# The sample's attention and heads in other steps of a two-layer hybrid decoder step

## The chip, the cores and the metric

The kernel runs on one core of one Trainium2 chip. The metric is device time in microseconds (us) of one execution, lower is better. Engines: TensorE (PE, its weight loads PEld), VectorE (DVE), ScalarE (ACT), GpSimd (POOL), and SyncE (SP), which here issues every load and store as one queue, in order. The granted clock of TensorE is given as a share of its full 2.4 GHz.

## The reference, cut to what matters

Two layers, each with a prompt of 2048 tokens and a "sample" of 8 sequences with 4 tokens each, on the same weights (D_MODEL 1024):

```
z = rms(x) @ w_in                       # 1024 -> 3336 columns
att = sink attention (window 128: the prompt banded, the sample against its cache) * silu(gate_a)
dn  = gated delta rule over conv(q, k, v): chunks of 64, a unit triangular solve per
      chunk and head, then a scan over the chunks; rms norm * silu(gate_d)
y = x + concat(att, dn) @ w_out
```

The prompt has 32 chunks and four delta heads. The sample runs the same formulas on its cached keys and its recurrent state. Layer 2 needs layer 1's sample output as its input, so layer 1's sample work has to be done before layer 2's sample products begin. Layers are called 0 and 1 below.

## The kernel before, in words

The prompt is worked in groups of 512 tokens: four groups a layer, g0 to g3 for layer 0, g4 to g7 for layer 1, one after the other. A group is 68 steps. Each step takes a piece of the weights (two in each of the first four) and issues 12 main products with it (24 in the first four, L484; each fp32 product is three, on high and low halves). The steps by block: 0–3 k, v and the delta coefficients; 4–11 the delta branch's k; 12–19 the attention's q; 20–27 the delta q; 28–35 the delta v; 36–43 the delta gate; 44–51 the attention gate; 52–67 w_out.

Weights: in the first group of a layer the raw piece is loaded (L259) and split into `hl` by ScalarE (L262) and GpSimd (L263), and hl goes to DRAM (L273). The other groups load hl back (L265, 512 KB a piece). Piece n is used in step n − 4 (from piece 8 on). hl has five buffers, so the load of piece n waits until TensorE is done with piece n − 5, which is step n − 9. In the rows of the order below, `hl_4884<-hl0_34_1603` is the load of piece 34 of layer 0.

All else hangs on these steps. `tk.add(gen, n, s, e)` spreads the n parts of a generator over steps s to e, and the table W holds the numbers. In which row an instruction then stands on its engine is settled when the program is built, by a scheduler that also weighs when each buffer comes free: small tiles come from shared pools (f2, nine buffers; f4, five).

For each group one chain is of weight: the gate products (L607), pre (L762 to L781: its matrices AK), stores to `ad` (L788), two loads At on SP (L805), 31 rows of the triangular inverse on GpSimd (L811, L813), X (L817), the store xd and the loads Xc and Xd on SP (L824 to L829), and on TensorE the first product that joins the inverse's blocks, L840, called p1 below. What follows needs the inverse: more joins, the scan over chunks, the norm and gate, and w_out's second half.

The sample's work stands between. `SampleProducts` (L519) multiplies the sample's x with each raw piece. Sample attention, pre (its conv and gates) and four heads (`sample_head`) follow. Its output products (smT, L519 again) need the raw pieces of w_out. The heads' matmuls are those of L1275 to L1343, sample attention is L1097 to L1169, sample pre L1193 to L1247.

The lines that this turns on:

```
add(inv_rows(), 33, W["ir0"], W["ir1"][gi])
add(inv_task(), 6, W["iv0"][gi], W["iv1"][gi])
...
hl = wp.tile([P, 2, kk, m], F32R, tag="hl", name="hl", bufs=W["wla"] + 1)
...
dma(At[r], ad.rearrange("a b j i -> (a b) j i"))
...
dma(xd.rearrange("a b i j -> (a b) i j"), X)
Xd = f2([P, NC, 32], name="Xd")
dma(Xd, xd.rearrange("a b i j -> (b i) a j"))
```

Of the kernel before, what the change touches and what calls it, by code (L numbers as in the profile page):

```python
# [18 lines left out]
P = 128  # L19
# [3 lines left out]
NB_S = 8  # L23
# [8 lines left out]
NG = SEQ // T  # L32
# [12 lines left out]
C_END = 512  # L45

W = dict(k1=8, pre0=13, pre1=19, q0=17, q1=30, ir0=20, ir1=((32,) + (27,) * 3), iv0=(36, 31, 31, 31), iv1=(41, 36, 36, 36), att0=24, att1=47,
         qk0=29, qk1=35, sc0=(41,) * 4, sc1=52, sa0=-4, sa1=30, sp0=20, sp1=50, sh0=58, shd=11, shl=13, wla=4, wraw=3, xn0=2, xn1=8, sla=3,
         md0=53, md1=55, ma0=45)


R3 = 3 * TS
# [89 lines left out]
def hybrid_kernel(ctx, tc, a):  # L142
# [20 lines left out]
    def f4(shape, dt=F32, name="f4"):  # L163
        return f4p.tile(shape, dt, tag="f4", name=name, bufs=5)

    def f2(shape, dt=F32, name="f2"):
        return f2p.tile(shape, dt, tag="f2", name=name, bufs=9)
# [7 lines left out]
    def xt_(shape):  # L175
        return ps_x.tile(shape, F32, tag="x", name="px")
# [30 lines left out]
    def silu2(out, z, n, m):  # L207

        th = f2([P, m], name="th")
        A.activation(th[:n], z, AF.Tanh, scale=0.5)  # L210
        V.scalar_tensor_tensor(out, th[:n], 1.0, z, op0=ALU.add, op1=ALU.mult)
# [22 lines left out]
    def pieces():  # L234
        for l in range(DEPTH):
            stash = []
            for gi in range(NG):
                for n, (src, out) in enumerate(pieces_of(l)):
                    if gi == 0:
                        kk, m = src.shape[1:]  # L240
                        stash.append(dr.tile([P, 2, kk, m], F32, name=f"hl{l}_{n}"))
                    yield src, stash[n], gi == 0, gi == 0 or (gi == 2 and out)

    wsrc = pieces()
    wready = []

# [30 lines left out]
    tk = Tasks()  # L277
# [253 lines left out]
    def sample_projections(L, sT):  # L531
        zcol = [0]

        def zstore(zt):
            n = zt.shape[1]
            dma(L.zs[:, zcol[0]:zcol[0] + n], zt)
            zcol[0] += n

        return SampleProducts(sT, [(W0C, 1, zstore)] + [(256, 2, zstore) if feat else (512, 1, zstore) for feat, _ in BLOCKS])
# [529 lines left out]
    def s1(shape, nm):  # L1069
        return smt(shape, nm, 1)  # L1070
# [190 lines left out]
    def sample_head(L, h):  # L1261
        l, zs, n = L.l, L.zs, TS
        kT, qT, vT = (y[:, h] for y in L.kqv)
        hs = slice(h, h + 1)
        hw = f2([R3, 4, P], name="hw")
        r, o = hw[:, 0], hw[:n, 3:4]
        S0 = f4([P, NB_S, P], name="S0")
        dma(S0, a["state_delta"][l, :, h].rearrange("b k v -> k b v"))
        dg = f2([n, P], name="dgs")
        dma(dg, zs[:, Z_DG + h * P:Z_DG + (h + 1) * P])  # L1270
        sel = f2([P, 2, P], name="sel")
        dma(sel, a["const_k"])
        yield
        pa = xt_([n, 2, n])
        PE.matmul(pa[:, 0], kT[:, 0:n], kT[:, 0:n], start=True, stop=True)  # L1275
        PE.matmul(pa[:, 1], kT[:, 0:n], qT[:, 0:n], start=True, stop=True)
        AKs = s1([n, 2, 3, n], "AKs")
        for i in range(2):
            V.scalar_tensor_tensor(AKs[:, i], pa[:, i].unsqueeze(1).to_broadcast([n, 3, n]), L.scc[:n, hs],
                                   L.dec[:, h].unsqueeze(1).to_broadcast([n, 3, n]), op0=ALU.mult, op1=ALU.mult)  # L1280
        V.tensor_mul(AKs[:, 0], AKs[:, 0], cs_s[:n, S_STR:S_STR + n].unsqueeze(1).to_broadcast([n, 3, n]))
        kq = f2([P, NB_S, 32], name="kq")
        G.memset(kq, 0.0)
        for i, y in enumerate((kT, qT)):
            V.tensor_copy(kq[:, :, LS * i:LS * i + LS], y.rearrange("p (b l) -> p b l", l=LS))
        kv3 = f2([P, 2, 3, n], name="kv3")
        A.copy(kv3[:, 0], kT.unsqueeze(1).to_broadcast([P, 3, n]))
        A.copy(kv3[:, 1], vT.unsqueeze(1).to_broadcast([P, 3, n]))
        yield

        pkq = xt_([P, 2, P])
        for b in range(NB_S):
            r0 = 32 * (b % 4)
            PE.matmul(pkq[r0:r0 + 32, b // 4], kq[:, b], S0[:, b], start=True, stop=True, tile_position=(0, r0))
        kqs = f2([P, 2, P], name="kqs")
        A.copy(kqs, pkq)
        yield
        pt = xt_([P, 3, P])
        for hb in range(2):
            PE.matmul(pt[:, 0], sel[:, hb], kqs[:, hb], start=(hb == 0), stop=(hb == 1))  # L1300
        for i in range(2):
            PE.transpose(pt[:R3, 1 + i], kv3[:, i].rearrange("p a b -> p (a b)"), ident)
        V.tensor_scalar(r, pt[:R3, 2], L.ssqv[:, hs], None, op0=ALU.mult)
        V.scalar_tensor_tensor(r, pt[:R3, 0], L.neG[:, hs], r, op0=ALU.mult, op1=ALU.add)
        V.tensor_copy(o[:, 0], pt[R3:, 0])
        V.tensor_scalar(o[:, 0], o[:, 0], L.eG[:n, hs], None, op0=ALU.mult)
        kd = f2([R3, P], name="skd")
        V.tensor_scalar(kd, pt[:R3, 1], L.sck[:, hs], None, op0=ALU.mult)
        kd3 = wk.tile([R3, P], F32R, tag="kd3", name="kd3", bufs=1)
        V.tensor_copy(kd3, kd)  # L1310
        V.tensor_sub(kd3[n:2 * n], kd[n:2 * n], kd3[n:2 * n].bitcast(F32))
        yield
        w = r
        for i in range(LS - 1):
            pm = xt_([R3, P])
            PE.matmul(pm, AKs[:, 0].rearrange("p a b -> p (a b)"), w[:n], start=True, stop=True)
            w2 = hw[:, 1 + i % 2]
            V.tensor_sub(w2, r, pm)
            w = w2
            yield  # L1320
        pm = xt_([n, P])
        PE.matmul(pm, AKs[:, 1, 0], w[:n], start=True, stop=True)
        V.tensor_add(o[:, 0], o[:, 0], pm)
        w3 = wk.tile([R3, P], F32R, tag="w3", name="w3", bufs=1)
        V.tensor_copy(w3, w)
        V.tensor_sub(w3[2 * n:3 * n], w[2 * n:3 * n], w3[2 * n:3 * n].bitcast(F32))
        wbd = f4([R3, NB_S, P], F32R, name="wbd")
        V.tensor_mul(wbd, w3.bitcast(F32).unsqueeze(1).to_broadcast([R3, NB_S, P]),
                     BM.unsqueeze(2).to_broadcast([R3, NB_S, P]))
        yield  # L1330
        for hb in range(2):
            pu = xt_([P, 4, P])
            PE.matmul(pu, kd3, wbd[:, 4 * hb:4 * hb + 4], start=True, stop=True)
            for b in range(4):
                bb = 4 * hb + b
                V.scalar_tensor_tensor(S0[:, bb], S0[:, bb], L.glb[:, h, bb:bb + 1], pu[:, b], op0=ALU.mult, op1=ALU.add)
        dma(a["s_delta"][l, :, h].rearrange("b k v -> k b v"), S0)
        gate = f2([n, 1, P], name="sgate")
        silu2(gate[:, 0], dg, n, P)
        delta_out(o, L.srq[:n, hs], L.srq2[:n, hs], gate, o, n)  # L1340
        yield
        pt = xt_([P, n])
        PE.transpose(pt, o[:, 0], ident[:n, :n])  # L1343
        A.activation(L.smT[:, 4 + h], pt, AF.Copy, scale=L.dngh)
        yield


    xT, sx, x = [], [], []
    lgen = layer(0)
    L = next(lgen)  # L1350
    sg = sx_stage(L, sx)
# [20 lines left out]
    for l in range(DEPTH):  # L1372
        for gi in range(NG):
            at = tk.at
            if gi == 1:
                tk.add(sample_att(L), 10, at + W["sa0"], at + W["sa1"])
                tk.add(sample_pre(L), 11, at + W["sp0"], at + W["sp1"])
                for h in range(4):
                    s = at + W["sh0"] + W["shd"] * h
                    tk.add(sample_head(L, h), 10, s, s + W["shl"])  # L1380
            if gi == 0:
                sg = sample_projections(L, sx[0])
            g = group(L, gi, xT, sg if gi == 0 else None)
            at, xT, x, Ln, gn = tk.at, [], [], L, gi + 1
            if gi == NG - 1 and l < DEPTH - 1:
                lgen = layer(l + 1)
                Ln, gn = next(lgen), 0
                sx = []
                tk.add(sx_stage(Ln, sx), 4, at + 10, at + 16)
                tk.add(lgen, 1, at + 4, at + 8)  # L1390
            if gn < NG:
                tk.add(x_norm(Ln, gn, x), 7, at + W["xn0"], at + W["xn1"])
                for kh in range(2):
                    tk.add(x_scale(Ln, kh, x, xT), 4, at + 11 + 4 * kh, at + 15 + 2 * kh)
            out_proj(L, gi, g, L.smT if gi == 2 else None)
            L = Ln


# [61 lines left out]
```

## Time and profile before

| | |
|---|---|
| median of 3 runs | 2385.87 us (2385.57 to 2388.23) |
| profiled execution | 2384.89 us |
| its span (first to last instruction) | 2383.1 us |
| TensorE, VectorE, ScalarE, GpSimd busy | 93%, 69%, 38%, 19% |
| mean granted clock of TensorE | 0.972 |
| longest and shortest group | g0 318.9 us, g3 274.2 us |

The groups follow each other without a gap, so the time is the sum of their lengths, plus 21.5 us before the first main product. Times of instructions are counted from the span's start.

### The profile page before, as it was taken

What the parts mean: (1) busy time and instruction counts of PE and PEld (TensorE: products, weight loads), DVE (VectorE), ACT (ScalarE), POOL (GpSimd) and SP (SyncE); (2) the same over time, 40 slices, a digit from 0 to 9 for tenths busy, and PEclk for the clock granted to TensorE, in tenths of its full rate; (3) what the DMA queues carried; (4) which work ended last, traced back from release to release, by engine and by line L of the source; (5) the groups of instructions that cost most, each with busy time, mean ns of one, the idle gap of its engine ahead of it and who ended that gap; (6) DMA issues with size and microseconds to landing.
All of it is one profiled execution on the core that took longest, in us unless ns stands there. A gap on an engine that the chain in (4) does not pass through costs nothing.

```text
span 2383.1 us, 41057 instructions
## 1 busy us (share of the span) xinstructions
PE 2227.7 (93%) x14340; PEld 1771.6 (74%) x14340; DVE 1642.2 (69%) x5060; ACT 909.6 (38%) x2864; POOL 447.4 (19%) x732
## 2 busy tenths in 40 slices
PE   6989999879999899979999899999899989999799
PEld 5766788658887687867877677887688777788677
DVE  6677677577678764677656867778767787557663
ACT  3544523234233342334325445244432344323331
POOL 3272320400004000040023623104000130002100
PEclk9989999979999999989999999999999999999899
DMA  5654685514765348544566546854357534675236
GB/s 172 208 190 160 206 282 184 158 57 140 225 194 170 105 146 267 181 124 131 162 213 222 173 148 215 272 190 125 118 162 224 192 113 133 200 231 161 82 116 199
DMA packets 211298, 414.14 MB, mean 174 GB/s; under 512 B 61340, under 2 KB 89604, under 8 KB 211028
## 3 DMA queue, kind: packets, MB, share of 16 engines
q1 hardware_dynamic: 211092, 411.53, 53.4%
q8 instruction: 113, 1.85, 0.3%
q14 instruction: 93, 0.76, 0.1%
HBM read 312.84 MB, written 101.62 MB: 174 GB/s over the span
## 4 chain that ended last, share of the span: by engine, by line
PE 59%; DVE 8%; POOL 6%; DMA 3%; issue 2%; ACT 2%; SPq 0%; POOLq 0%; ACTq 0%; DVEq 0%
PE mm L484 40%; POOL Xh L813 3%; POOL pr L811 3%; PE px L711 2%; PE px L946 1%; PE px L954 1%; PE px L940 1%; PE px L926 1%; PE px L934 1%; PE px L701 1%; PE px L781 1%; DMA hl<-hl 1%; PE px L668 1%; PE px L519 1%; DVE vT L744 1%
## 5 line engine op out<-in xcount | busy, mean ns | idle before, releaser
L484 PE MATMUL mm<-xT,hl 128*128 128x512 f32 x3072 | 777.5, 403 | 4.1 <-POOL hl L263 3.8
L484 PEld LDWEIGHTS mm<-xT,hl 128*128 128x128 f32 x3072 | 571.0, 192 | 124.2 <-issue 6.7
L484 PE MATMUL mm<-hl,xT 128*128 128x512 f32 (+1 forms) x2304 | 511.2, 369 | 44.3 <-DVE rs_t L204 25.9
L484 PEld LDWEIGHTS mm<-hl,xT 128*128 128x128 f32 x2304 | 379.1, 192 | 114.4 <-issue 56.5
L263 POOL TENSOR_TENSOR hl<-raw,hl 128x512 fp32r<-128x512 f32 (+1 forms) x144 | 186.5, 1300 | 409.7 <-ACT hl L262 360.2
L811 POOL TENSOR_TENSOR pr<-At,Xh 128x126 f32<-128x126 f32 (+22 forms) x248 | 99.2, 400 | 580.1 <-DMA At<-ad 286.6
L484 PE MATMUL mm<-mixA,hl 128*128 128x512 f32 x768 | 187.9, 397 | 0.0
L484 PE MATMUL mm<-mixD,hl 128*128 128x512 f32 x768 | 181.6, 392 | 1.0 <-DVE mixD L970 1.0
L1029 POOL TENSOR_TENSOR mixA<-m,mixA 128x256 fp32r<-128x256 f32 x64 | 45.5, 736 | 719.2 <-ACT mixA L1028 492.7
L484 PEld LDWEIGHTS mm<-mixD,hl 128*128 128x128 f32 x768 | 142.6, 188 | 33.7 <-DVE mixD L970 1.8
L744 DVE SCALAR_TENSOR_TENSOR KQ<-mm,pc,KQ 128x511 f32<-128x511 f32 (+2 forms) x192 | 142.0, 740 | 35.1 <-ACT KQ L741 34.8
L484 PEld LDWEIGHTS mm<-mixA,hl 128*128 128x128 f32 x768 | 140.7, 188 | 30.4 <-issue 2.2
L262 ACT CAST hl<-raw 128x512 fp32r<-128x512 f32 (+1 forms) x144 | 85.0, 595 | 140.2 <-PE mm L484 76.4
L689 ACT ACTIVATE Pt<-Pt,nm 128x128 f32<-128x128 f32 x256 | 99.3, 391 | 21.5 <-DVE nm L681 21.5
L813 POOL TENSOR_TENSOR Xh<-Xh,pr 128x126 f32<-128x126 f32 (+22 forms) x248 | 103.0, 416 | 18.9
L1060 DVE TENSOR_TENSOR xr<-mm,xr 128x512 f32<-128x512 f32 x64 | 43.7, 691 | 79.6 <-PE mm L484 79.6
L672 ACT COPY Pt<-px 128x256 f32<-128x256 f32 x128 | 43.7, 374 | 143.1 <-PE px L669 110.8
L704 DVE TENSOR_TENSOR PT<-px,cst 128x512 f32<-128x512 f32 x124 | 82.1, 683 | 16.7 <-PE px L701 16.2
L701 PE MATMUL px<-cst,Pt 128*128 128x128 f32 x256 | 41.9, 289 | 41.2 <-ACT th L210 26.9
L741 ACT ACTIVATE KQ<-mm,pc 128x512 f32<-128x512 f32 x64 | 43.7, 687 | 94.0 <-PE mm L484 93.9
L668 PE MATMUL px<-kT,q 128*128 128x256 f32 (+1 forms) x256 | 72.6, 313 | 5.0 <-DVE q L650 1.7
L359 ACT CAST xT<-x 128x512 fp32r<-128x512 f32 x64 | 35.5, 618 | 93.9 <-PE mm L484 83.0
(392 smaller groups left out, 3708.7 us busy)
## 6 DMA issues: line engine op xcount, KB each, us to landing
hl<-hl SPq DMA_DIRECT2D x512, 512.0 KB
hl<-hl SPq DMA_DIRECT2D x64, 264.0 KB
raw<-in_wf_dram SPq DMA_DIRECT2D x64, 256.0 KB
raw<-in_w_out_dram SPq DMA_DIRECT2D x64, 256.0 KB
x<-in_x_prompt_dram SPq DMA_DIRECT2D x16, 512.0 KB
raw<-in_wt_dram SPq DMA_DIRECT2D x32, 256.0 KB
xr<-in_x_prompt_dram SPq DMA_DIRECT2D x32, 256.0 KB
y<-xr SPq DMA_DIRECT2D x32, 256.0 KB
```

The lines of the kernel that those rows point to most:

```text
L262: A.copy(hl[:, 0], raw)
L263: G.tensor_sub(hl[:, 1], raw, hl[:, 0].bitcast(F32))
L484: PE.matmul(pss[u], lhs, rhs, start=(k == 0 and q == 0), stop=(k == 7 and q == 2))
L668: PE.matmul(sps[kv][:, jj, c0:], q, kT[:, kv, cols], start=True, stop=False)
L689: A.activation(Pt[:, kv, j], Pt[:, kv, j], AF.Exp, bias=nm[:, h:h + 1], scale=0.125, accum_out=den[:, h:h + 1])
L701: PE.transpose(pt[:, j, :], Pt[:, kv, j], ident)
L704: V.tensor_mul(ptt, pt, (umat if kb else slower).unsqueeze(1).to_broadcast([P, 4, P]))
L711: PE.matmul(po[kv * HD:kv * HD + HD, :], vts[tt + kb][:, kv * HD:kv * HD + HD], PT[kv, kb].rearrange("p a b -> p (a b)"), start=(kb == 0 o ...
L744: V.scalar_tensor_tensor(dest[:, d:], ps[:, 0:T - d], w, dest[:, d:], op0=ALU.mult, op1=ALU.add)
L811: G.tensor_mul(pr, At[:, j, j + 1:].unsqueeze(2).to_broadcast([P, n, m]), Xh[:, j, 0:m].unsqueeze(1).to_broadcast([P, n, m]))
L813: G.tensor_sub(Xh[:, j + 1:, 0:m], Xh[:, j + 1:, 0:m], pr)
L1029: G.tensor_sub(lo, m, hi.bitcast(F32))
```

## The change

- Sample attention, pre and heads of layer l now run from group l + 1 of the layer (g1 in layer 0, g6 in layer 1); before, from group 1 in both (g1, g5). In layer 0, attention and pre are spread over other, earlier steps (`sa1` 30 to 12, `sp0`, `sp1` 20, 50 to 8, 24), and the heads start 57, 66, 125 and 134 steps after the group's start, so two in each of the next two groups, each over 11 steps (before 58, 69, 80, 91, over 13). In layer 1 they start at 57, 66, 75 and 84. All those steps are clear of the blocks of v and the delta gate (28 to 43).
- The sample's input products of layer 1 move from g4 to g5. There the weights are not split, so the raw pieces are loaded once more, beside hl (13.4 MB).
- The output products move from the third group of a layer to the last (g2 to g3, g6 to g7), with their raw loads.
- The sample's x of layer 1 (`sx_stage`) is set up in steps 24 to 40 of g4, instead of 10 to 16 of g3.
- In each head five f2 tiles (kq, kv3, kqs, skd, dgs) are packed into two (kqv, kqd).

```diff
-         ... sa1=30, sp0=20, sp1=50, sh0=58, shd=11, shl=13, ...
+         ... sa1=12, sp0=8, sp1=24, sh=((57, 66, 125, 134), (57, 66, 75, 84)), shl=11, sx0=24, sx1=40, ...
...
-                    yield src, stash[n], gi == 0, gi == 0 or (gi == 2 and out)
+                    yield src, stash[n], gi == 0, gi in (0, 3) if out else gi in (0, l)
...
-        dg = f2([n, P], name="dgs")
+        kqv = f2([P, 512], name="kqv")
+        kq = kqv[:, 0:256].rearrange("p (b l) -> p b l", l=32)
+        kv3 = kqv[:, 256:448].rearrange("p (i a b) -> p i a b", i=2, a=3)
+        kqd = f2([P, 512], name="kqd")
+        kqs = kqd[:, 0:256].rearrange("p (a b) -> p a b", a=2)
+        kd, dg = kqd[:R3, 256:384], kqd[:n, 384:512]
...
-            if gi == 1:
+
+            if gi == l + 1:
                 tk.add(sample_att(L), 10, at + W["sa0"], at + W["sa1"])
                 tk.add(sample_pre(L), 11, at + W["sp0"], at + W["sp1"])
                 for h in range(4):
-                    s = at + W["sh0"] + W["shd"] * h
+                    s = at + W["sh"][l][h]
                     tk.add(sample_head(L, h), 10, s, s + W["shl"])
-            if gi == 0:
-                sg = sample_projections(L, sx[0])
-            g = group(L, gi, xT, sg if gi == 0 else None)
+            if gi == 0 and l == 1:
+                sx = []
+                tk.add(sx_stage(L, sx), 4, at + W["sx0"], at + W["sx1"])
+            sg = sample_projections(L, sx[0]) if gi == l else None
+            g = group(L, gi, xT, sg)
...
-            out_proj(L, gi, g, L.smT if gi == 2 else None)
+            out_proj(L, gi, g, L.smT if gi == NG - 1 else None)
```

The rows move as follows at the three places that the prediction speaks of.

On SP in g1, before, around the two At loads (hl0_33 is piece 33 of layer 0):

```order
L265 DMA hl_4713<-hl0_31_1441 128x1024
L265 DMA hl_4742<-hl0_32_1476 128x1024
L265 DMA hl_4798<-hl0_33_1534 128x1024
L805 DMA At_4509<-ad_4159 64x1024
L265 DMA hl_4884<-hl0_34_1603 128x1024
L805 DMA At_4509<-ad_4159 64x1024
L265 DMA hl_4948<-hl0_35_1685 128x1024
```

and of the change:

```order
L265 DMA hl_5583<-hl0_42_2111 128x1024
L265 DMA hl_5705<-hl0_43_2212 128x1024
L265 DMA hl_5728<-hl0_44_2252 128x1024
L788 DMA ad_4298<-AK_4297 32x4x32 x4
L805 DMA At_4663<-ad_4298 64x1024 x2
L824 DMA xd_5326<-X_5046 64x1024
L828 DMA Xc_5330<-xd_5326 32x16x32
L829 DMA Xc_5330<-xd_5326 32x16x32
L826 DMA Xd_5328<-xd_5326 128x16x32
L265 DMA hl_5748<-hl0_45_2321 128x1024
```

Both At loads move behind the load of piece 44, ten pieces later, and the store and loads of the inverse's result follow at once.

On SP in g5, before, around the same loads (hl1 is layer 1):

```order
L265 DMA hl_17048<-hl1_28_13809 128x1024
L788 DMA ad_16682<-AK_16681 32x4x32
L265 DMA hl_17101<-hl1_29_13866 128x1024
L805 DMA At_17032<-ad_16682 64x1024
L265 DMA hl_17155<-hl1_30_13898 128x1024
L805 DMA At_17032<-ad_16682 64x1024
L265 DMA hl_17236<-hl1_31_13964 128x1024
```

and of the change, with the raw pieces between:

```order
L265 DMA hl_16953<-hl1_31_13761 128x1024
L259 DMA raw_16992<-in_wf_dram 128x512
L805 DMA At_16774<-ad_16412 64x1024
L259 DMA raw_17053<-in_wf_dram 128x512
L265 DMA hl_16994<-hl1_32_13786 128x1024
L265 DMA hl_17055<-hl1_33_13839 128x1024
L259 DMA raw_17125<-in_wf_dram 128x512
L805 DMA At_16774<-ad_16412 64x1024
```

The second At load moves from piece 30 to piece 33, and behind raw loads.

On TensorE in g1, before, from the group's first block on (96 products of 264 columns are steps 0 to 3, then 12 a step):

```order
L484 MATMUL mm<-hl,xT 128x264 x96
L484 MATMUL mm<-xT,hl 128x512 x33
L607 MATMUL px<-cst,gx 128x128
L617 MATMUL px<-g,cst 128x16
L618 MATMUL px<-g,ones 128x16
L484 MATMUL mm<-xT,hl 128x512 x15
```

and of the change:

```order
L484 MATMUL mm<-hl,xT 128x264 x72
L1097 MATMUL px<-cst,qks 128x32
L1099 MATMUL px<-cst,qks 128x32 x4
L484 MATMUL mm<-hl,xT 128x264 x24
L484 MATMUL mm<-xT,hl 128x512 x96
L484 MATMUL mm<-hl,xT 128x512 x3
L1112 MATMUL px<-cst,kc 128x128 x8
L607 MATMUL px<-cst,gx 128x128
```

The gate product L607 moves behind the sample attention's key transposes, from 33 main products into the K block to 99, the first of step 12.

## Rows read from the trace of the kernel before

**Rows 1.** The page: the span, and busy time, share and instructions by engine.

```profile
span 2383.1 us, 41057 instructions
...
PE 2227.7 (93%) x14340; PEld 1771.6 (74%) x14340; DVE 1642.2 (69%) x5060; ACT 909.6 (38%) x2864; POOL 447.4 (19%) x732
```

**Rows 2.** Windows, groups g0 to g7; columns as printed in the first line.

```profile
core 0: us, PE busy (x) PEld busy (x) DVE busy (x) ACT busy (x) POOL busy (x), PEclk, DMA share, GB/s
21.50:340.40 318.90, 294.72 (x1999) 225.42 (x2000) 223.50 (x580) 144.27 (x418) 121.95 (x141) 0.96 0.59 201
340.40:645.20 304.80, 280.39 (x1740) 226.16 (x1738) 206.36 (x707) 104.74 (x346) 31.84 (x73) 0.94 0.49 157
645.20:940.50 295.30, 283.14 (x1824) 223.54 (x1824) 213.57 (x697) 105.83 (x349) 34.22 (x75) 0.98 0.56 175
940.50:1214.70 274.20, 258.05 (x1589) 212.77 (x1587) 183.15 (x558) 101.15 (x325) 34.03 (x75) 0.98 0.52 162
1214.70:1527.60 312.90, 292.32 (x2023) 222.50 (x2023) 216.90 (x572) 142.66 (x415) 122.25 (x141) 0.97 0.60 201
1527.60:1812.30 284.70, 274.30 (x1741) 221.55 (x1739) 206.84 (x704) 105.02 (x346) 32.66 (x73) 0.99 0.52 164
1812.30:2107.60 295.30, 283.13 (x1823) 223.72 (x1823) 213.56 (x697) 105.76 (x349) 35.27 (x75) 0.98 0.55 174
2107.60:2383.10 275.50, 255.81 (x1564) 210.80 (x1562) 165.20 (x506) 91.38 (x304) 31.25 (x72) 0.97 0.48 152
```

**Rows 3.** Timeline of SP's issues, g1, g2, g4, g5, g7: start, us, instruction.

```profile
430.36 0.48 SPq L805 DMA_DIRECT2D At<-ad  x1
...
462.21 0.32 SPq L265 DMA_DIRECT2D hl<-hl  x1
...
475.45 0.48 SPq L829 DMA_DIRECT2D Xc<-xd  x1
...
491.36 0.38 SPq L826 DMA_DIRECT2D Xd<-xd  x1
...
724.74 0.46 SPq L805 DMA_DIRECT2D At<-ad  x1
...
1308.70 0.47 SPq L805 DMA_DIRECT2D At<-ad  x1
...
1601.19 0.47 SPq L805 DMA_DIRECT2D At<-ad  x1
...
2178.30 0.45 SPq L805 DMA_DIRECT2D At<-ad  x1
```

**Rows 4.** Timeline of TensorE at p1 in the same groups: start, us, instruction.

```profile
498.41 1.20 PE L840 MATMUL px<-Xd,AK 32*32 32x32 f32 x64
...
791.22 1.20 PE L840 MATMUL px<-Xd,AK 32*32 32x32 f32 x64
...
1401.27 1.20 PE L840 MATMUL px<-Xd,AK 32*32 32x32 f32 x64
...
1665.74 1.14 PE L840 MATMUL px<-Xd,AK 32*32 32x32 f32 x60
...
2245.08 1.20 PE L840 MATMUL px<-Xd,AK 32*32 32x32 f32 x64 [0.25 <-DMA Xd<-xd]
```

**Rows 5.** Windows: g1 before p1; first 20 steps of g2, g3; eight steps.

```profile
462.20:490.20 28.00, 9.70 (x41) 7.66 (x41) 20.84 (x63) 12.97 (x54) 2.95 (x5) 0.59 0.17 42
...
645.20:718.60 73.40, 73.40 (x452) 60.32 (x451) 56.40 (x229) 26.42 (x95) 0.62 (x2) 1.00 0.68 204
...
940.50:1005.30 64.80, 64.46 (x380) 55.70 (x379) 38.51 (x146) 23.85 (x80) 0.00 (x0) 1.00 0.63 200
...
952.30:975.80 23.50, 23.16 (x107) 18.95 (x107) 17.29 (x74) 7.77 (x17) 0.00 (x0) 1.00 0.66 214
```

**Rows 6.** Groups of instructions by line, L519: busy us, mean ns.

```profile
L519 PE MATMUL px<-raw,sxT 128*32 128x128 f32 (+1 forms) x896 | 48.0, 288 | 0.8 <-DMA raw<-in_wf_dram 0.5 <-DMA raw<-in_w_dram 0.4
...
L519 PE MATMUL px<-raw,smT 128*32 128x128 f32 x256 | 12.8, 283 | 0.5 <-DMA raw<-in_w_out_dram 0.5
```

More of the change, by code (lines that the diff above doesn't have):

```diff
@@ L47 @@
 W = dict(k1=8, pre0=13, pre1=19, q0=17, q1=30, ir0=20, ir1=((32,) + (27,) * 3), iv0=(36, 31, 31, 31), iv1=(41, 36, 36, 36), att0=24, att1=47,
-         qk0=29, qk1=35, sc0=(41,) * 4, sc1=52, sa0=-4, sa1=30, sp0=20, sp1=50, sh0=58, shd=11, shl=13, wla=4, wraw=3, xn0=2, xn1=8, sla=3,
+         qk0=29, qk1=35, sc0=(41,) * 4, sc1=52, sa0=-4, sa1=12, sp0=8, sp1=24, sh=((57, 66, 125, 134), (57, 66, 75, 84)), shl=11, sx0=24, sx1=40, wla=4, wraw=3, xn0=2, xn1=8, sla=3,
          md0=53, md1=55, ma0=45)
@@ L1281, in sample_head @@
         V.tensor_mul(AKs[:, 0], AKs[:, 0], cs_s[:n, S_STR:S_STR + n].unsqueeze(1).to_broadcast([n, 3, n]))
-        kq = f2([P, NB_S, 32], name="kq")
         G.memset(kq, 0.0)
@@ L1285, in sample_head @@
             V.tensor_copy(kq[:, :, LS * i:LS * i + LS], y.rearrange("p (b l) -> p b l", l=LS))
-        kv3 = f2([P, 2, 3, n], name="kv3")
         A.copy(kv3[:, 0], kT.unsqueeze(1).to_broadcast([P, 3, n]))
@@ L1294, in sample_head @@
             PE.matmul(pkq[r0:r0 + 32, b // 4], kq[:, b], S0[:, b], start=True, stop=True, tile_position=(0, r0))
-        kqs = f2([P, 2, P], name="kqs")
         A.copy(kqs, pkq)
@@ L1306, in sample_head @@
         V.tensor_scalar(o[:, 0], o[:, 0], L.eG[:n, hs], None, op0=ALU.mult)
-        kd = f2([R3, P], name="skd")
         V.tensor_scalar(kd, pt[:R3, 1], L.sck[:, hs], None, op0=ALU.mult)
@@ L1387, in hybrid_kernel @@
                 Ln, gn = next(lgen), 0
-                sx = []
-                tk.add(sx_stage(Ln, sx), 4, at + 10, at + 16)
                 tk.add(lgen, 1, at + 4, at + 8)
```

## The prediction

> **What bounds the kernel now.** The page comes first: TensorE is busy for 93% of the span, VectorE for 69%, GpSimd for 19% [rows 1]. That looks like a kernel that its matmuls pace, and for most of a group they do. The table by group is read next [rows 2]: every group has the same 864 main products, yet the lengths go from 274.2 us (g3) to 318.9 us (g0). Two things make the difference. Part is more work on TensorE (the busy column: 258.05 in g3, 283.14 in g2). The rest is time in which it stands still: length less busy is 139.7 us over the eight groups (2361.6 less 2221.9, the sums of the two columns), 24.4 in g1, 10.4 in g5, 24.2 and 20.6 in g0 and g4.
>
> To see what TensorE waits for, follow one chain: the second At load on SP, then 31 rows of the inverse on GpSimd, X, xd, Xd, and the first join product p1 (L840) on TensorE. The starts are in [rows 3] and [rows 4]. From At to p1 it takes 68.0 us in g1 (430.36 to 498.41), 66.5 in g2, 64.5 in g5 and 66.8 in g7; g3 and g6 have the form of g7 and g2. Where the weights are split it takes 92.6 (g4), since GpSimd also does the subtractions of the split (122.25 us busy there, against 31 to 35 elsewhere [rows 2]). So the window is nearly the same whatever else a group does: who moves the At load moves p1, and TensorE cannot go past p1, as its queue is in order. From p1 to the group's end it is 146.8 us in g1, 149.3 in g2, 126.3 in g4, 146.6 in g5 and 138.0 in g7 (group ends from [rows 2]). A group is thus three stretches: start to At, the window, and the tail.
>
> That the window does stop TensorE is seen in g1: in the 28 us from 462.20 it is busy for 9.70, and the granted clock is 0.59, which is a mix of 2.4 GHz (1.0) and 1.2 GHz (0.5) [rows 5].
>
> **Prices.** A sample head's matmul: the first 20 steps of g2 take 73.40 us and those of g3 64.80 [rows 5]; they differ by 41 sample matmuls, so 8.6/41 = 0.21 us each, evictions and waits included. The sample's output products are 12.8 us busy over both layers, 6.4 us a layer; its input products are 48.0, so 24 a layer [rows 6]. Little hides them, since they stand in TensorE's queue between main products and TensorE is busy there for 73.40 of 73.40 us.
>
> **The change group by group** (all against the profiled execution, 2384.89 us, 0.04% below the median of 2385.87).
>
> *g0* is the same program: 0.
>
> *g1: +26.* The sample's attention and pre are now spread over steps up to 24 and its heads are gone. That should help TensorE; the order says otherwise. The gate product L607 moves from step 6 to 12, the prompt's pre products from 13–19 to 19–32, and SP issues both At loads behind the load of piece 44, not around that of piece 34 (the first place of the order). SP is in order, and piece 44's load needs the buffer of piece 39, which TensorE frees at the end of step 35. Before, that load left at 462.21 [rows 3]. After, some 30 small matmuls (transposes and scores of q) that stood ahead of it follow it; at the 0.1 to 0.2 us above that is about 5 us, so 457 (452 to 465). Then four small stores to ad, which At reads, and the two At loads: about 6 us by the distances of such issues, At at 463 instead of 430.36. With 66 to 68 us of window p1 stands at 530, 31 later. The tail loses 19 sample matmuls, 4 us: 146.8 − 4. Sum 31.6 − 4 = +27; at the lower end of the window (66) +26, which I take. Were piece 44 no obstacle, the last pre product in step 32 (10 us earlier) would hold At at about 453, and the sum would be +16.
>
> *g2: −12, g3: +11.* The output products leave g2 for g3, and of the heads two stand in each, by 20 and 22 matmuls in the order that reach into them, with At back where g3 has it now, behind piece 30. g2 = g3 of before with 42 sample matmuls: 274.2 + 42·0.21 = 283.0, against 295.3. g3 = 274.2 + 22·0.21 + 6.4 = 285.2.
>
> *g4: −22.* The 24 us of input products leave. The split stays, so the window stays at 92.6 and only what stood before At and in the tail is saved, but that is nearly all: idle of 20.6 us (312.9 − 292.3) bounds what may be swallowed. Range −17 to −38, the latter if the idle time of this group, too, came from the products.
>
> *g5: +17.* It gets the 24 us of products and the raw weights again, 13.4 MB, and loses sample attention and heads. At stands behind pieces 31 and 33 and two raw loads, thus three steps later (second place of the order): 3·2.94 us (the eight steps from 952.30 take 23.50 [rows 5]), 120 of the 224 products stand ahead of At, at 24/224 = 0.107 us each 12.8, some 25 sample matmuls fewer are −5: +16.7. Window 66.5 rather than 64.5: +2. Tail: 64 products come (6.9), 43 sample matmuls go (9.0): −2. Range +12 to +31, the upper end if the raw loads make the weights late. Their room: 164 GB/s over 284.7 us is 46.7 MB; with 13.4 more in 302 us it is 199 GB/s, and g0 moves 201 [rows 2]. That is the only evidence on contention, and it bounds the cost: g0 is also the group with the longest window.
>
> *g6: −1.* Sample attention and pre of layer 1 come, with one head; output products (6.4) go; the order has 100 sample matmuls there instead of 62, 38 at 0.1 to 0.21 are about 5. The order of its inverse stays.
>
> *g7: +20.* The heads and the output products come; the order of its SP and TensorE reads like that of g2 of before, so 295.3 against 275.5.
>
> Sum: 26 − 12 + 11 − 22 + 17 − 1 + 20 = +39, so **2424 us**. Total work is the same but for the second raw load; what is lost is g1's window, which is opened 33 us late with nothing left to fill it. The moves of the other groups nearly cancel (+13).
>
> **Rivals.**
>
> *The window shrinks (other side).* The change packs five f2 tiles of each head into two (kqv, kqd), and in g1 the order has xd, Xc, Xc and Xd in one piece. Before, in g1, Xd is issued at 491.36, 15.9 us after the second Xc at 475.45 [rows 3]: SP waited for a buffer. If it now leaves at once, each window shrinks, by at most 15.9 us. Seven groups take part (all but g0); it decides from 39/7 = 5.6 us each, and 10 us each give 2354. Against it: Xd in the order of after still waits for VectorE and TensorE, which release its buffer. The Trainium skill, "Perfetto Trace Analysis", section "Optimization Strategy", says that the same gap repeated can mean too few buffers; here a gap of the same size does repeat, but no row shows that the buffer is the packed tiles'.
>
> *TensorE sets the time.* Its main products do not change, and it is at 93% [rows 1]. If its queue has enough to do in the longer g1 window, work moves and the sum does not: 2384.9 ± 5. For it: all that is moved is TensorE work that exists in both programs. Against it: lengths in [rows 2] do not go with busy time (g3 and g5, 16.2 busy apart, are 10.5 apart in length; g1 has 6 more than g5 and is 20.1 longer). The Trainium skill, "Perfetto Trace Analysis", section "Identifying the Most-Contended Engine", would put the engine with the highest occupancy first, and by it the time would not move; for TensorE the same section warns that matmul busy share is not a measure of headroom, and the trace bears the warning out.
>
> *Heavier.* g5's raw loads and g1's queue of weight loads behind xd starve TensorE after p1 as well, and g4's window keeps what its products cost: g4 −17, g5 +31, g1 +31: 2448.
>
> **How the numbers follow.** The forecast has 0.66, the shrinking window 0.10, TensorE as the limit 0.08, the heavier case 0.16. The forecast's own spread is about ±15 (g1 ±8, g4 and g5 ±8 each). The range reaches up over the heavier case to 2454, and down to 2394, where half a shrunken window and g1's +16 would put it. What a measurement can tell from no change is some 0.2%, 4.8 us. Faster by more: 0.09 (the shrinking window, nearly all). Within: 0.10 (the limit, and the shrinking window at 5 to 6 us). Slower: 0.81.
>
> **What would show it.** In g1 the second At at about 463 and p1 at about 530, TensorE idle for some 45 us just before p1 with the clock down; from 424 to 450 there is no At load at all. Group lengths about 319, 331, 283, 285, 291, 302, 294, 295. At to p1 of 64 to 68 us in the unsplit groups. The forecast is wrong if At in g1 leaves by 445, if g1's window is under 58 us, or if g7 stays below 285.

## The result and the profile after

The changed kernel takes 2427.17 us (median of 4 runs, 2423.97 to 2427.23) against 2386.01 us of the kernel before: ratio 1.0167, 95% interval 1.0150 to 1.0185. It is 1.7% slower; the forecast was 2424.

The page of the changed kernel, span and engines, answers to [rows 1]:

```profile
span 2425.4 us, 41072 instructions
...
PE 2236.6 (92%) x14340; PEld 1778.9 (73%) x14340; DVE 1639.1 (68%) x5060; ACT 913.6 (38%) x2864; POOL 440.2 (18%) x732
```

TensorE has the same number of instructions, and its busy share falls by about one point only, though 42 us were lost. The windows by group, of the changed kernel, answer to [rows 2] (same columns):

```profile
21.70:342.40 320.70, 295.67 (x1998) 226.49 (x1999) 225.81 (x595) 144.95 (x419) 121.04 (x141) 0.95 0.58 199
342.40:676.10 333.70, 287.92 (x1759) 231.90 (x1758) 208.79 (x721) 107.55 (x350) 32.02 (x74) 0.92 0.47 146
676.10:959.00 282.90, 267.65 (x1654) 217.61 (x1652) 197.76 (x625) 101.85 (x333) 32.24 (x74) 0.97 0.54 163
959.00:1245.80 286.80, 270.51 (x1731) 216.78 (x1731) 190.95 (x587) 103.32 (x335) 34.31 (x76) 0.97 0.56 172
1245.80:1530.90 285.10, 263.13 (x1608) 215.29 (x1606) 213.03 (x552) 137.67 (x388) 119.55 (x140) 0.98 0.65 217
1530.90:1833.40 302.50, 284.59 (x2014) 220.96 (x2003) 187.77 (x591) 104.80 (x347) 30.47 (x72) 0.97 0.62 194
1833.40:2130.00 296.60, 280.35 (x1760) 224.62 (x1758) 207.78 (x715) 107.41 (x351) 32.70 (x74) 0.97 0.51 158
2130.00:2425.40 295.40, 280.94 (x1789) 220.18 (x1788) 194.18 (x635) 97.24 (x331) 33.92 (x74) 0.98 0.54 166
```

The lengths against those of [rows 2], with the forecast's terms:

| | g0 | g1 | g2 | g3 | g4 | g5 | g6 | g7 | sum |
|---|---|---|---|---|---|---|---|---|---|
| measured | +1.8 | +28.9 | −12.4 | +12.6 | −27.8 | +17.8 | +1.3 | +19.9 | +42 |
| forecast | 0 | +26 | −12 | +11 | −22 | +17 | −1 | +20 | +39 |

So g1 makes two thirds of the loss; in g2 to g5 and g7 gains and losses of 12 to 28 us cancel for the most part, and the seven other groups together leave 13. In g1 length less busy, which is TensorE's idle time, grew from 24.4 to 45.8 us (333.70 − 287.92), and its clock fell from 0.94 to 0.92.

Timeline of SP in g1 of the changed kernel, answering to [rows 3] (start, us, instruction, count):

```profile
464.79 0.32 SPq L265 DMA_DIRECT2D hl<-hl  x1
465.21 1.80 SPq L788 DMA_DIRECT2D ad<-AK  x4
469.28 1.15 SPq L805 DMA_DIRECT2D At<-ad  x2
504.63 0.46 SPq L824 DMA_DIRECT2D xd<-X  x1
507.57 0.31 SPq L828 DMA_DIRECT2D Xc<-xd  x1
507.93 0.48 SPq L829 DMA_DIRECT2D Xc<-xd  x1
508.51 0.44 SPq L826 DMA_DIRECT2D Xd<-xd  x1
```

The load of piece 44 leaves at 464.79; only then the last stores to ad and the two At loads, the second at 469.84: 127.4 us after the group's start, where it was 90.0. That is the queue that was read from the order. But the end of the list is not as thought: Xd leaves 0.58 us after Xc, no longer 15.9 after it, and still the join comes 23 us later. What TensorE waits for is seen in its own timeline of g1 (the bracket is idle time before the instruction and what ended it):

```profile
475.86 1.44 PE L1247 MATMUL px<-ones,ssq 128*96 128x1 f32 x8 [11.09 <-ACT ssq L1245]
...
510.28 1.09 PE L701 MATMUL px<-cst,Pt 128*128 128x128 f32 x4 [20.37 <-DVE Pt L696]
...
522.27 2.04 PE L484 MATMUL mm<-hl,xT 128*128 128x512 f32 x4 [5.05 <-ACT Pt L689]
...
531.98 1.20 PE L840 MATMUL px<-Xd,AK 32*32 32x32 f32 x64
```

The join (L840) itself waits for nothing. TensorE's longest stop is at L701, the turn (transpose) of the attention's probabilities Pt. ScalarE and GpSimd of the same stretch say why:

```profile
502.95 0.65 ACT L672 COPY Pt<-px 128x256 f32<-128x256 f32 x2 [4.11 <-POOL pr L811]
```

```profile
502.70 0.22 POOL L811 TENSOR_TENSOR pr<-At,Xh 128x16 f32<-128x16 f32 x1
```

ScalarE copies the next scores into Pt 0.03 us after GpSimd's last row has read At. Pt and At are both f4 tiles, of a pool with five buffers. The copy uses none of the tiles of GpSimd's row, and At is the only f4 tile among them, so Pt gets the buffer of At. A late At therefore holds up the softmax, the softmax the turn L701, and all that stands behind L701 in TensorE's queue, main products of steps 36 and on among it, stands too.

The second stop, 11.09 us at L1247, has the same root by the other pool. L1247 is a product of the sample's pre, which the change has moved ahead of step 36. It waits for the squares ssq, an f2 tile, and ScalarE starts on them 0.03 us after GpSimd's second row:

```profile
475.28 0.52 ACT L1245 ACTIVATE ssq<-skqv 128x384 f32<-128x384 f32 x1 [14.95 <-POOL Xh L813]
```

```profile
474.99 0.26 POOL L813 TENSOR_TENSOR Xh<-Xh,pr 128x30 f32<-128x30 f32 x1
```

That row has just read an f2 tile (pr), so ssq waited for a buffer that the inverse's rows could free only after At had come. The two stops are 31.5 of the 45.8 us.

The tie between At and Pt is not new. In g3 of the kernel before, ScalarE's copy into Pt waits in the same way, and TensorE stands at L701:

```profile
1046.99 0.37 ACT L672 COPY Pt<-px 128x256 f32<-128x256 f32 x1 [13.74 <-POOL pr L811]
```

```profile
1053.06 1.09 PE L701 MATMUL px<-cst,Pt 128*128 128x128 f32 x4 [13.47 <-ACT th L210]
```

### The profile page after: what moved, and what is told of

The parts are those of the page before. It is cut to its first block, busy times and chain, and to the rows that moved or that the text cites. A ratio compares the mean times of both kernels' runs of the same rounds, so it can differ in the third digit from the quotient of the medians.

```text
span 2425.4 us, 41072 instructions
## 1 busy us (share of the span) xinstructions
PE 2236.6 (92%) x14340; PEld 1778.9 (73%) x14340; DVE 1639.1 (68%) x5060; ACT 913.6 (38%) x2864; POOL 440.2 (18%) x732
## 4 chain that ended last, share of the span: by engine, by line
PE 74%; DVE 9%; POOL 5%; DMA 4%; issue 4%; ACT 3%; SPq 0%; POOLq 0%; ACTq 0%; DVEq 0%
PE mm L484 51%; PE px L711 2%; POOL Xh L813 2%; POOL pr L811 2%; PE px L519 2%; PE px L781 1%; PE px L701 1%; PE px L946 1%; DMA hl<-hl 1%; PE px L954 1%; DVE vT L744 1%; PE px L940 1%; DVE KQ L744 1%; PE px L668 1%; PE px L926 1%
## 5 line engine op out<-in xcount | busy, mean ns | idle before, releaser
L701 PE MATMUL px<-cst,Pt 128*128 128x128 f32 x256 | 42.4, 291 | 79.2 <-DVE Pt L696 65.7
L813 POOL TENSOR_TENSOR Xh<-Xh,pr 128x126 f32<-128x126 f32 (+22 forms) x248 | 103.5, 417 | 19.2 <-DVE rs_t L203 0.2
L701 PEld LDWEIGHTS px<-cst,Pt 128*128 128x128 f32 x256 | 31.7, 148 | 88.0 <-issue 68.8
```

The source lines that it names most:

```text
L701: PE.transpose(pt[:, j, :], Pt[:, kv, j], ident)
L813: G.tensor_sub(Xh[:, j + 1:, 0:m], Xh[:, j + 1:, 0:m], pr)
```

## The experiments

All runs are set against runs of the kernel before on the same chip; that kernel's medians lay between 2385.6 and 2388.5. "At" and "p1" below are the starts of the second At load and of L840, counted from the group's first main product.

**1. Layer 0's spread put back.**

```diff
-tk.add(sample_att(L), 10, at + W["sa0"], at + W["sa1"])
-tk.add(sample_pre(L), 11, at + W["sp0"], at + W["sp1"])
+tk.add(sample_att(L), 10, at + W["sa0"], at + (30, W["sa1"])[l])
+tk.add(sample_pre(L), 11, at + (20, W["sp0"])[l], at + (50, W["sp1"])[l])
```

> The changed kernel with the spread of layer 0's sample attention and pre put back to the old steps (to 30, and 20 to 50); heads, products and packing stay changed. In its order the second At load of g1 stands behind piece 34 again. Theory (the new spread in layer 0 delays At in g1 and that is the loss): g1 falls from 333.7 to about 304 us and the rest stays, 2427.2 - 29 = 2398. Rival (the loss comes from the second raw load or from the heads' places): g1 falls by less than 8, time 2420 or more.

Measured: 2399.68 us, ratio 1.0063 (1.0048 to 1.0079). The window of g1 in that run:

```profile
342.55:649.42 306.87, 282.34 (x1759) 227.06 (x1757) 212.30 (x736) 106.42 (x352) 32.62 (x74) 0.94 0.50 157
```

The two spreads (three numbers of W) carry 27.5 of the 41 us, and g1 is back at 306.9. The rest of the change costs 0.6%.

**2 and 3. One of the two spreads each.** Only the first, or only the second, of the two lines above.

> The changed kernel with only the attention's spread of layer 0 put back (to step 30); pre stays at 8 to 24. In its order the gate product of g1 is back in step 6, but the last pre product of the prompt stands in step 34 and At behind piece 44. Theory (the start of At sets p1): as the changed kernel, 2427 +- 6, with At in g1 at 466 to 473. Rival (the late gate product delays the chain): 2400 to 2410.

> The changed kernel with only the sample pre's spread of layer 0 put back (20 to 50); attention stays at up to 12. In its order the gate product of g1 stays in step 12, but the last pre product of the prompt stands in step 19 and At behind piece 40 (step 31). Theory (At sets p1, and p1 the group): At at about 452 to 456, 14 to 18 us earlier than 469.8, time 2410 to 2414. Rival (the gate product decides): 2427 +- 5. Second rival (p1 does not follow At): 2398 or 2427.

Measured: attention old 2418.24 us, ratio 1.0133 (1.0107 to 1.0159); pre old 2412.52 us, ratio 1.0109 (1.0086 to 1.0132). The starts in the run with attention old, SP and then TensorE (the run began g1 at 339.94):

```profile
458.58 1.15 SPq L805 DMA_DIRECT2D At<-ad  x2
```

```profile
519.57 1.20 PE L840 MATMUL px<-Xd,AK 32*32 32x32 f32 x64
```

The second came out as expected, with At at 110.1 and p1 at 172.2. The first was expected at 2427 ± 6 and was 9 us faster, so that expectation missed: step 35 ended at 114.2 instead of 122.3, and At left at 119.2. At and p1 move together in both, and each spread alone delays g1. The gate product's place does not decide by itself: with it back in step 6 (the first) At is later than with it in step 12 (the second).

**4. The inverse's stores and loads on another queue.** In the changed kernel, in the groups that don't split weights:

```diff
-dma(ad[...], AK[...])
+(dma if gi == 0 else nc.gpsimd.dma_start)(ad[...], AK[...])
...
-dma(At[r], ad...)
+(dma if gi == 0 else nc.gpsimd.dma_start)(At[r], ad...)
```

> The changed kernel with the stores to ad and the At loads issued from GpSimd's queue in the groups that do not split weights, so that they no longer stand behind weight loads on SP; layer 0's spread stays changed. Theory (two parts delay At in g1: the pre products, which end at 454.9, and SP's wait for the buffer of piece 44, about 10 us): g1 shortens by about 8 to 10, the other groups by 0 to 5 each, time 2400 to 2418. Rival (SP's queue holds nothing that the pre products do not hold): 2427 +- 4. Against both: a slower store from that queue, 2430 to 2440.

Measured: 2379.96 us, ratio 0.9976 (0.9966 to 0.9985): 47 us less than the changed kernel, far more than expected. Windows of g1, g2 and g5 of that run:

```profile
341.83:661.31 319.48, 284.53 (x1760) 228.96 (x1758) 209.80 (x721) 107.54 (x351) 42.13 (x92) 0.94 0.49 152
661.31:937.03 275.72, 267.03 (x1654) 217.70 (x1653) 198.85 (x625) 102.04 (x333) 42.80 (x92) 0.99 0.54 168
1503.10:1791.94 288.84, 283.80 (x2008) 219.88 (x2003) 189.19 (x592) 105.15 (x347) 42.49 (x90) 0.99 0.63 203
```

g1 loses 14.2 us (At at 114.8), where 8 to 10 were expected, and its stop at L1247 is gone. g5 loses 13.7, since At no longer stands behind weight and raw loads (82.3 instead of 95.3); g2 and g3 7.2 and 5.2, though At left only 0.8 earlier there: their stretch from At to p1 shortened from 67 to 61 and 63. g6 loses 4.8. TensorE's rows at L701 in g2, of the changed kernel and of this run, show where the stretch shortened:

```profile
791.72 1.09 PE L701 MATMUL px<-cst,Pt 128*128 128x128 f32 x4 [13.29 <-DVE Pt L696]
```

```profile
766.39 1.09 PE L701 MATMUL px<-cst,Pt 128*128 128x128 f32 x4 [3.50 <-DVE Pt L696]
```

In g3 that stop falls from 13.50 to 4.44 us, in g5 from 9.86 to 4.03. In g2 and g3 of this run the softmax that L701 needs stands ahead of ScalarE's copy that waits for At's buffer; in the changed kernel it stands behind it. The edit thus changed the order of ScalarE's rows too, as the order is made anew when the program is built, and its gain is not that of the queue alone.

**5. The same on the kernel before.**

> The kernel before, with the stores to ad and the At loads issued from GpSimd's queue in the groups that do not split weights. Theory (At's start sets p1 and p1 the group's end): in g1 the last pre product ends 64.3 us after the group's start and At leaves at 90.0; from the other queue At leaves at about 72 to 75, so g1 shortens by 15 to 18; g5 from 73.6 to about 72, g2, g3, g6 and g7 by the 4 to 7 that their windows lost in the changed kernel. Sum 2386 - 35 = 2351 (2340 to 2365). Rival (buffers of f4 hold At, not SP's queue): 2380 to 2386.

Measured: 2369.71 us, ratio 0.9927 (0.9913 to 0.9940). The gain is half of what was expected: g1 loses 6.3 us, g3 4.7 and g7 7.1, g2, g5 and g6 next to nothing. In g3 and g7 the stop at L701 falls from 13.5 us to 6.0 and 3.5. There, too, the copy that waits for At's buffer now follows the turn. At in g1 left at 73.9, 16.1 earlier, as expected; p1 came only 6.4 earlier, at 151.6. Its row carries no wait:

```profile
494.81 1.20 PE L840 MATMUL px<-Xd,AK 32*32 32x32 f32 x64
```

TensorE reaches that place of its queue no sooner: its longest stops ahead of p1 in g1 are 4.4, 4.1 and 2.3 us, and none is at L701. So p1 is bound there by what stands ahead of it in TensorE's queue, and not by At.

**6. Both on the changed kernel: old spread and the other queue.**

> The changed kernel with layer 0's old spread and with ad and At on GpSimd's queue. If the two delays of g1 are independent, the gains add: 2427.2 - 27.5 (old spread alone) - 47.2 (queue alone) = 2352, less if g1 is not delayed twice by the same thing. Theory (both act on the same start of At in g1, the queue also on the other groups): g1 to about 287 to 292, the rest as with the queue alone: 2380 - 28 = 2352. Rival (in g1 At is held by a buffer until about 90 us): g1 near 305, 2365 to 2368.

Measured: 2362.61 us, ratio 0.9899 (0.9885 to 0.9912). The gains don't add in full, for the reason of 5: g1 is 300.2, with At at 73.6 and p1 at 151.2. It is faster than the kernel before with the same queue by some 7 us; the new places of heads, output products and layer 1's products are then no loss.

**7. The same with xd, Xc and Xd on that queue too.**

> The changed kernel with layer 0's old spread and with ad, At and also the store xd and the loads Xc and Xd on GpSimd's queue in the groups that do not split. If SP's queue still holds Xd: p1 earlier by 2 to 6 in g2, g3 and g5 to g7, where TensorE has reached its place, and 2340 to 2355 instead of 2362.6. If TensorE's own row order holds p1: 2362.6 within 4.

Measured: 2363.80 us, ratio 0.9891 (0.9877 to 0.9906): no difference from 6. SP did not hold Xd where it mattered.

**8. All of layer 0's places put back**, only layer 1 and the packing changed (`sh` of layer 0 58 to 91 over 13 steps, `L.smT if gi == l + 2`, the spread of 1).

> The changed kernel with all of layer 0's places put back (spread, heads, output products in the third group); layer 1 and the packing stay changed. Theory (layer 0 loses 31 us, layer 1 about 11): 2386 + 11 = 2397, and g0 to g3 within 2 us each of the kernel before. Rival (the heads' new places and the output products in the last group cost something too): under 2392.

Measured: 2398.52 us, ratio 1.0046 (1.0031 to 1.0062), g0 to g3 320.4, 305.2, 296.1 and 273.6. Layer 1 and the packing cost 0.46%, about 11 us; the forecast's terms for g4 to g7 sum to 14.

**9. The packing alone on the kernel before.**

> The kernel before with only the packing of the heads' five f2 tiles into two. Theory (Xd waits for VectorE and TensorE, not for the heads' tiles): 2386 within 4, At to p1 in 64 to 68 us. Rival (the packing frees buffers, so Xd leaves earlier): each of six windows 5 to 15 shorter, 2300 to 2356.

Measured: 2390.90 us, ratio 1.0012 (1.0003 to 1.0020). At to p1 is 64.6 to 68.8 in the unsplit groups, as before. The rival that lived on the packed tiles is gone.

**10. The same lateness elsewhere.** The kernel before, in g5 alone:

```diff
-add(inv_rows(), 33, W["ir0"], W["ir1"][gi])
-add(inv_task(), 6, W["iv0"][gi], W["iv1"][gi])
+add(inv_rows(), 33, W["ir0"] + 8 * (L.l == gi == 1), W["ir1"][gi] + 8 * (L.l == gi == 1))
+add(inv_task(), 6, W["iv0"][gi] + 5 * (L.l == gi == 1), W["iv1"][gi] + 5 * (L.l == gi == 1))
```

> The kernel before with one thing moved: in g5 the inverse's rows are asked for 8 steps later and its join 5 steps later, so that the order has At behind piece 38 (end of step 29) instead of piece 30, and p1 at the start of step 40 instead of in step 37. Theory (At's start sets p1, and p1 the rest of the group): At later by about 23 us, p1 later by 18 to 24, g5 longer by 12 to 22 (some of the three steps' work now stands ahead of p1), 2400 to 2408. Rival (there is other work for TensorE in the meantime): g5 longer by less than 5.

Measured: 2394.04 us, ratio 1.0021 (1.0011 to 1.0032). At, p1 and the group in that run:

```profile
1639.76 0.47 SPq L805 DMA_DIRECT2D At<-ad  x1
```

```profile
1701.31 1.20 PE L840 MATMUL px<-Xd,AK 32*32 32x32 f32 x64
```

```profile
1532.99:1824.21 291.22, 277.72 (x1741) 224.56 (x1739) 206.72 (x704) 104.96 (x346) 30.30 (x73) 0.97 0.50 160
```

At left 33.2 us later in the group and p1 came 30.2 later, yet g5 grew by 6.5 only: from p1 to the group's end it was 122.9 instead of 146.6. Neither the theory (12 to 22) nor the rival (under 5) came true. Work that followed p1 before now stands ahead of it and fills the wait, so a late At need not cost its lateness.

**11. The second raw load alone.** The kernel before, with layer 1's raw input pieces loaded in g5 and used by nothing: `gi == 0 or (gi == 2 and out) or (l == gi == 1 and not out)`.

> The kernel before with the raw input weights of layer 1 loaded again in g5 (13.4 MB), used by nothing; the order of At and p1 stays. Theory (contention costs little as the DMA share of g5 goes from 0.52 to about 0.6, which g0 has): g5 longer by 0 to 3, 2386 to 2390. Rival (the second raw load is a large part of g5's loss of 18): g5 longer by 8 or more.

Measured: 2440.75 us, ratio 1.0211 (1.0192 to 1.0229), g5 334.3 instead of 284.7. Windows from its first steps:

```profile
1536.00:1567.00 31.00, 16.80 (x100) 15.18 (x99) 8.10 (x40) 4.81 (x13) 0.00 (x0) 0.83 0.86 278
1567.00:1619.00 52.00, 29.80 (x111) 22.84 (x110) 19.70 (x91) 6.47 (x13) 0.00 (x0) 0.74 0.84 274
```

This doesn't measure the changed kernel's load. With no reader to pace them, up to three raw loads stand ahead of each hl load on SP, and TensorE starves in steps 0 to 11: in these 83 us it waits 19.2 us for hl loads, and 13.8 us for VectorE, which itself waited for stores of the group before, issued from the same queue. In the changed kernel, where each raw piece waits for its products, the first 44 us of g5 show as high a DMA share and no such hunger:

```profile
1531.00:1547.00 16.00, 15.19 (x156) 13.16 (x152) 3.39 (x9) 3.35 (x11) 0.00 (x0) 1.00 0.82 248
1547.00:1575.00 28.00, 28.00 (x181) 19.98 (x179) 19.06 (x81) 9.05 (x22) 0.00 (x0) 1.00 0.89 296
```

TensorE is busy for 43.19 of 44.00 us there. So 13.4 MB more cost 50 us when they all go first; what they cost over the whole group when they are paced was not measured by itself.

**12. A late At, with work to do.** The changed kernel, in g1 alone, the scores and the join asked for later:

```diff
-add(inv_task(), 6, W["iv0"][gi], W["iv1"][gi])
-add(att_task(), 20, W["att0"], W["att1"])
+add(inv_task(), 6, W["iv0"][gi] + 5 * (gi == 1 and L.l == 0), W["iv1"][gi] + 5 * (gi == 1 and L.l == 0))
+add(att_task(), 20, W["att0"] + 12 * (gi == 1 and L.l == 0), W["att1"])
```

> The changed kernel with two things asked for later in g1 alone: the prompt's attention scores by 12 steps and the inverse's join by 5. In its order At stays behind piece 44, but the main products of steps 36 to 39 stand ahead of the first turn of the probabilities (L701) and of p1, which moves from step 37 to step 40. Theory (a late At costs what TensorE's row order makes it cost: TensorE stood behind L701, whose Pt waits for the buffer that At holds, with the products of steps 36 to 39 ready behind it): TensorE's idle time in g1 falls from 45.8 by 10 to 18 us, g1 from 333.7 to 316 to 324, time 2409 to 2417, with At where it was. Rival (a late At costs its lateness wherever the join stands): 2427 +- 5.

Measured: 2410.16 us, ratio 1.0097 (1.0081 to 1.0114), 17 less than the changed kernel. The window of g1:

```profile
342.17:658.88 316.71, 284.80 (x1760) 228.11 (x1758) 208.04 (x721) 107.07 (x351) 31.89 (x74) 0.94 0.50 153
```

At left at 127.6, as late as in the changed kernel, and g1 is 17.0 shorter, with 31.9 us of idle time instead of 45.8. The rival falls. The stop at L701 is gone, a new one of 10.08 us stands at L893, and that at L1247 is still there (11.20 us), as the sample's pre was not moved.

The runs of g1 side by side:

| kernel | At | p1 | length of g1 |
|---|---|---|---|
| 6, old spread and other queue | 73.6 | 151.2 | 300.2 |
| 5, before with other queue | 73.9 | 151.6 | 298.5 |
| before | 90.0 | 158.0 | 304.8 |
| 1, old spread | 89.9 | 158.0 | 306.9 |
| 3, pre old | 110.1 | 172.2 | 321.2 |
| 4, other queue | 114.8 | 175.8 | 319.5 |
| 2, attention old | 119.2 | 179.6 | 323.0 |
| changed | 127.4 | 189.5 | 333.7 |
| 12, scores and join later | 127.6 | 184.7 | 316.7 |

As long as the order of scores, turn and join stays, each us of At from 90 on costs 0.6 to 0.8 us (28.9 over 37.4 in the changed kernel, 18.2 over 29.2 in 2); what else stands ahead of p1 differs a little from run to run. Below 90 an earlier At gains less (6.3 over 16.1 in 5). The last row leaves that line.

## Why the prediction was right, and where it was not

**The sum.** 2424 against 2427.17; every group's term came within 6 us, and seven of the eight within 3. In g1 and g5 a part of that is luck, as the parts of the term missed in opposite directions.

**g1.** What At stands behind was read right from the order: the last pre product ended at 454.9 and SP was held by piece 44 until 464.79. The size was off: At left at 469.84 against "463", as step 35 ended no sooner in the group than before (122.3 us after its start, before 121.8), so the 5 us that the moved matmuls should save there are missing. The window was 62.1 us against the 66 to 68 of the forecast. The two misses cancel, and p1 came at 531.98 against 530. Experiments 1 to 3 show that the new spread makes this, both parts of it, and experiment 4 that SP's queue is a part of it (At 12.6 us earlier without it, 4.2 of which is an earlier end of the pre products). The step that failed is "TensorE cannot go past p1": the stops were not at p1 but ahead of it, 20.37 us at L701, which waits for the buffer that At holds, and 11.09 us at L1247, which waits for one that the inverse's rows hold. The sum was blind to that, since the window from At to p1 contains both. It matters for the remedy: experiments 10 and 12 show that a late At costs less where TensorE has products to do ahead of the turn or the join. "From p1 to the group's end" is no constant either (146.6 and 122.9 us in g5, for two orders).

**g2, g3, g6, g7.** Confirmed within 2.3 us. In g7 the parts came true as well: At at 78.4 and p1 at 146.2, against 79.5 and 146.0 in g2 of before. But the price of a sample head's matmul was read wrong: the two windows of [rows 5] differ by 72 matmuls (452 less 380), all of the heads, and not by 41, so it is 8.6/72 = 0.12 us. The counts taken from the order were short too (42 in g2, where the trace has 74), and the product of the two came out right there. With the trace's counts g2 is 274.2 + 74·0.12 = 283.1 as before; g3, with 23, is 283.4, 3.4 us short of the measured 286.8; and g6, with 64 more, is +1.3, as measured.

**g4.** −27.8 against −22. "The window stays at 92.6" was wrong: it is 83.0 (1324.80 to 1407.85), and 83.0 to 84.4 in every run in which the products have left g4, against 91.9 to 93.7 in those in which they stay. What in them lengthens it was not tested. The range given, −17 to −38, held the result.

**g5.** +17.8 against +17, by the way that was forecast, with the parts off: At came 21.7 us later (95.3 instead of 73.6) and not 16.7, the window grew by 1.7 against 2, and the tail gave back 5.6 and not 2. Experiment 4, where At is off SP, takes 13.7 of the 17.8 away. The price of the raw load by itself stays open, as experiment 11 measured another thing; the row of TensorE's first 44 us only bounds it there.

**The rivals.** The packing did not shrink the windows (experiment 9); that of g1 is 62.1 in the changed kernel, but 68.0 in experiment 1, which has the packing too. TensorE was not the limit: its count of instructions stayed and the time rose by 1.7%. Of the heavier case only g1, at +28.9, shows a trace; g4 went the other way. The rule on repeated gaps and too few buffers ("Perfetto Trace Analysis" of the Trainium skill, section "Optimization Strategy") speaks of a gap on the engine that should be saturated. The prediction put it to a gap on SP, that of Xd, which went away in g1 without making g1 shorter. On TensorE of the kernel before the trace agrees with the rule: the stop at L701 repeats, 13.47 us in g3 and 13.46 in g7, while Pt waits for an f4 buffer. A larger f4 or f2 pool, which would test it directly, was not tried.

**The version to keep** is that of experiment 6, 1.0% faster than the kernel before (0.9899, 0.9885 to 0.9912).

## What to carry to other kernels

When a change moves work that shares an in-order queue with a long chain, find the load that opens the chain in the new order, and name what its queue entry stands behind: here one load, 37 us later, made two thirds of the loss, and moving it, with the stores that it reads, to the queue of an engine that is busy for 19% (GpSimd) won 0.7% even without the change, part of it by another order of ScalarE's rows. A late opening costs what stands behind the first instruction of the bottleneck engine that waits, so look for that one, and not for the one that seems to need the result. Tiles of two chains that share a pool tie the chains together.

## What the runs showed of the hardware

- A load issued from GpSimd's queue is no slower in g1: two At loads take 1.06 us to issue there (1.15 on SP), and GpSimd starts on them 3.65 us after that (3.57 from SP, in the changed kernel), by its own rows in experiment 4:

```profile
456.11 1.06 POOL L805 DMA_DIRECT2D At<-ad  x2 [1.77 <-DMA ad<-AK]
460.82 0.58 POOL L811 TENSOR_TENSOR pr<-At,Xh 128x31 f32<-128x31 f32 x1 [3.65 <-DMA At<-ad]
```

- The granted clock follows the stops: in the 76 us around L701 of the changed kernel TensorE was busy for 35.59 us at 0.69 (a mix of 1.2 and 2.4 GHz), so a stop also makes the small products behind it slower. One score product takes 0.41 us in the stretch from 481.60 to 489.90, where the granted clock is 0.50, and 0.28 in experiment 12, where it is 1.00.

```profile
457.00:533.00 76.00, 35.59 (x223) 30.38 (x221) 45.26 (x146) 25.44 (x84) 25.72 (x64) 0.69 0.19 51
```

- Loads of 274 to 278 GB/s ran beside a TensorE that starved (experiment 11) and of 296 GB/s beside one that was always busy (g5 of the changed kernel), so the rate by itself does not decide.
